# Layer-1 sparse-attention mixer rewritten: scores in fp32 on half arrays, four head-branches per unit, other fillers

## The chip, the core and the metric

One Trainium2 chip, of which the program uses one core. The metric is the device time of one execution in microseconds (us); the time before is 1038.02 us, the median of three runs (1037.85 to 1038.6). TensorE is called PE here, its weight loads PEld, VectorE DVE, ScalarE ACT, SyncE's DMA queue SP.

## The reference, cut to what matters

A two-layer decoder trunk in fp32 on 256 tokens of width 1024. Only the mixer of layer 1 changes:

```python
def mixer_nsa(h, in_w, cmp_pos, cmp_w1, cmp_w2, out_w, pos):     # 16 heads in 2 groups, head size 64
    u = h @ in_w
    q, kc, vc, ks, vs, kw, vw, gl = jnp.split(u, cuts, axis=-1)
    q_rope = rope_partial(q, pos)
    kcmp, vcmp = compress(kc, ...), compress(vc, ...)            # 15 compressed blocks
    gates = jax.nn.sigmoid(gl)                                   # three per head
    ...
    o_c = softmax(q @ kcmp, masked) @ vcmp
    o_s = softmax(q_rope @ rope(ks), causal) @ vs                # with 256 tokens all blocks are selected
    o_w = softmax(q_rope @ rope(kw), causal) @ vw                # and the window of 512 holds them all
    y = gates[0] * o_c + gates[1] * o_s + gates[2] * o_w
    return y @ out_w
```

So a head has two full causal branches ("selected" and "window") and one short compressed one. Around the mixer, in both layers, stand adaLN-modulated SwiGLU feed-forwards whose weights stream from HBM.

## The kernel before

All large products are done as three matmuls in fp32r (`mm3`, L154): each weight piece of 128x1024 is split by `Stream.step` (L76) into a high part `wh` (ACT, L86) and a rest `wl` (DVE, L90), each activation into HH and HL or yh and yl, and high x high, high x low and low x high are summed in PSUM. The split pieces lie in seven slots (`SPL_BUFS`), the raw ones in seven more. Attention products (`y<-pt,nvp`, transposes) are plain fp32; such a matmul shows as two PE instructions, called passes here, and two weight loads.

The tile framework orders the instructions of each engine itself from the order in the program and from what is ready; only blocks under `in_order()` keep the written order. `transition` (L371) is such a block: between two stages it finishes the last output columns of the stage before (`steps[b]`), updates x, and starts four projections of the next stage (`group(k)`: 12 matmuls) before the RMS sums are known; the sums go to PE after `lag` groups. It first asks (`st.need(p0 + 4)`) for five weight pieces of the next stage.

`mixer1` (L921) runs, in program order: the transition; the query projections 0 and 1 (`proj2`); the token projections (values and gates, into `vb`); rope of the keys and their split into kh and kl, stacked so that the contraction has 128 rows; the compression MLP (`hidden`), woven into the query projections 2 and 3; the rope of the queries and their split (`stack_q`, `place_q`); query projections 4 to 6; the compressed scores. Then comes `attention` (L615) over 32 jobs (8 head pairs i x 2 groups g x 2 branches), a software pipeline of five steps: `scores` (for a pair of jobs four fp32r matmuls of 256 and 512 columns over K=128, then a DVE custom instruction that adds the mask and takes the minimum, L626), `exps` (ACT, L634), `norm` (DVE, L643), `trans` (three PE transposes, L650, and a copy out of PSUM, L653 or L655) and `pv` (`y`, two fp32 matmuls of 256 and 128 columns). After four jobs `done` adds the compressed branch and hands y[i] to `OutProj`, whose 8 x 8 blocks of three matmuls are the filler between jobs (`op.some`), as are query projection 7 and the second half of the compressed branch (`todo`).

PSUM has eight banks: two oa and two ob accumulators, and four more, in attention three `ps` and one `y`. `mixer0` (L747) uses the same `attention` with fp32 scores over K=64 (`ps<-qf,qf`), one head after another.

Of the kernel before, what the change touches and what calls it, by code (L numbers as in the profile page):

```python
# [117 lines left out]
def hybrid_trunk_kernel(ctx: ExitStack, tc: tile.TileContext, xT, c, wst, mst, prm_d, cst_d, wab_d, cw1_d, cw2_d,  # L118
# [8 lines left out]
    banks4 = ExitStack()  # L127
# [9 lines left out]
    banks_for("psp", 4, 0)  # L137
# [10 lines left out]
    def ob():  # L148
        return accp.tile([P, 512], F32, tag="ob", name="ob")
# [302 lines left out]
    def ffn(name, l, i, prev):  # L452
# [83 lines left out]
        else:  # L536
# [143 lines left out]
    def rope(z, ap):  # L680
        rp = ob()
# [65 lines left out]
    def mixer0(prev):  # L747
# [12 lines left out]
        with tc.tile_pool(name="lru", bufs=1) as lp:  # L760
# [17 lines left out]
            def unrope(w):  # L778
                scatter(qf[w], rope(z[w], lp))
# [141 lines left out]
    def mixer1(prev):  # L921
# [8 lines left out]
        qf = [mp.tile([P, 4, S], F32, name=f"nqf{w}") for w in range(2)]  # L930
        kf = mp.tile([P, 2, S], F32, name="kf")
        kh = mp.tile([P, 2, 2, S], F32R, name="kh")
        kl = mp.tile([P, 2, 2, S], F32R, name="kl")
        vp = mp.tile([P, 2, 2, 192], F32, name="nvp")
        G.memset(vp[:, :, :, 64:128], 0.0)
# [8 lines left out]
        hid = [mp.tile([P, 2, 16], F32, name=f"hid{w}") for w in range(2)]  # L944
        for w in range(2):
            G.memset(hid[w], 0.0)
        G.memset(zk, 0.0)
        nc.sync.dma_start(out=cw2, in_=cw2_d)

        def do_q(i, b):  # L950
            A.activation(out=qf[i // 4][:, i % 4], in_=b, func=ACTF.Copy, scale=0.125)
            if i % 4 == 3:
                gather(zq[i // 4], qf[i // 4])

        with tc.tile_pool(name="cmp", bufs=1) as cp:
# [12 lines left out]
            kx = cp.tile([P, 2, S], F32, name="kx")  # L968
            for g in range(2):
                nc.sync.dma_start(out=kx[64 - 64 * g:128 - 64 * g], in_=kc[64 * g:64 * g + 64])  # L970
            for w in range(2):
                for g in range(2):
                    r = 64 * g + w
                    nc.sync.dma_start(out=zk[r:r + 61:4], in_=kf[64 * g:64 * g + 16, w])
            do_q(0, b0[:, 0:S])
            do_q(1, b1[:, 0:S])
            vb = [ps(), ps()]
            for q in range(3):
                wh, wl = st.need(p0 + 6 + q)
                for k in range(3 * q, min(3 * q + 3, KD)):  # L980
                    sl = slice((k - 3 * q) * 304, (k - 3 * q) * 304 + 304)
                    for t in range(2):
                        ts = slice(t * P, (t + 1) * P)
                        o = vb[t][:, 0:304]
                        mm(o, HH[:, k, ts], wh[:, sl], k == 0)
                        mm(o, HH[:, k, ts], wl[:, sl], False)
                        mm(o, HL[:, k, ts], wh[:, sl], False, k == KD - 1)
                st.free(p0 + 6 + q)
            for t in range(2):
                A.activation(out=gts[:, t], in_=vb[t][:, 256:304], func=ACTF.Sigmoid)  # L990
                src = vb[t][:, 0:256].rearrange("p (a e d) -> p a e d", a=2, e=2)
                dv = vp[:, t].rearrange("p a (b d) -> p a b d", b=3)[:, :, 0:3:2, :]
                A.activation(out=dv, in_=src, func=ACTF.Copy)
            preload(ACTF.Gelu_apprx_tanh, gts[:, 1, 0:1])
            zr = rope(zk, cp)
# [4 lines left out]
            for g in range(2):  # L1000
                a, b = slice(64 * g, 64 * g + 64), slice(64 - 64 * g, 128 - 64 * g)
                A.activation(out=kh[a, g], in_=kf[a], func=ACTF.Copy)
                A.activation(out=kh[b, g], in_=kf[a], func=ACTF.Copy)
                V.tensor_tensor(out=kl[a, g], in0=kf[a], in1=kh[a, g].bitcast(F32), op=ALU.subtract)
                V.tensor_tensor(out=kl[b, g], in0=kf[a], in1=kh[a, g].bitcast(F32), op=ALU.subtract)
            x2 = []
            for w in range(2):
# [10 lines left out]
                x2.append(t)  # L1018
            hb = [ps(), ps()]
# [5 lines left out]

            for w in range(2):
                b = oa()
                proj(p0 + 9 + w, b[:, 0:S], [lambda w=w, q=q: hidden(w, q) for q in range(8)])
                do_q(2 + w, b[:, 0:S])
# [6 lines left out]
        qs = [ap.tile([P, 2, 4, S], F32R, name=f"qs{w}", bufs=1) for w in range(2)]  # L1036

        def stack_q(w, i0, i1):
            for g in range(2):
                a, b = slice(64 * g, 64 * g + 64), slice(64 - 64 * g, 128 - 64 * g)  # L1040
                src, hi = qf[w][a, i0:i1], qs[w][a, g, i0:i1]
                A.activation(out=hi, in_=src, func=ACTF.Copy)
                V.tensor_tensor(out=qs[w][b, g, i0:i1], in0=src, in1=hi.bitcast(F32), op=ALU.subtract)

        def rope_q(w):
            zr = rope(zq[w], ap)
            zs = [ap.tile([P, S], F32R, tag=t, name=t, bufs=1) for t in ("zh", "zl")]
            split(*zs, zr)
            return zs

        def place_q(w, zs):
            for e in range(2):
                for n in range(2):
                    r = 64 * (e ^ n)
                    move(qs[w][r:r + 16, e].rearrange("p i t -> p (i t)"), zs[n][64 * e:64 * e + 64])

        scb = {}

        def cmp_scores(i):
            w = i // 4  # L1060
            if i % 4 == 0:
                scb[w] = ob()
# [4 lines left out]
        def cmp_soft(w):  # L1067
            sc = ap.tile([P, 2, 8, 16], F32, tag="sc", name="sc", bufs=2)
# [19 lines left out]
        def cmp_trans(w, sc):  # L1088
            pt = ps()
            scf = sc.rearrange("p t h c -> p (t h c)")  # L1090
            for t in range(2):
                PE.transpose(pt[:, t * P:t * P + P], scf[:, t * P:t * P + P], ident)
            A.activation(out=pc[w], in_=pt[:, 0:2 * P], func=ACTF.Copy)

        zs = rope_q(0)
        stack_q(0, 0, 2)
        stack_q(0, 2, 4)
        place_q(0, zs)
        b = oa()
        proj(p0 + 11, b[:, 0:S])  # L1100
        do_q(4, b[:, 0:S])
        bk = ps()
        mm(bk[:, 0:32], cw2[:, 0], hid[0].rearrange("p g c -> p (g c)"), True, True)
        for g in range(2):
            rows, cols = slice(64 * g, 64 * g + 64), slice(16 * g, 16 * g + 16)
            A.activation(out=kbd[rows, cols], in_=bk[rows, cols], func=ACTF.Copy)
        hid4 = ap.tile([P, 4, 32], F32, name="hid4", bufs=1)
        V.tensor_copy(out=hid4, in_=hid[1].rearrange("p g c -> p (g c)").unsqueeze(1).to_broadcast([P, 4, 32]))
        b = oa()
        proj(p0 + 12, b[:, 0:S])  # L1110
        do_q(5, b[:, 0:S])
        for i in range(4):
            cmp_scores(i)
        sc0 = cmp_soft(0)
# [4 lines left out]
        b = oa()  # L1119
        proj(p0 + 13, b[:, 0:S])  # L1120
        do_q(6, b[:, 0:S])
        late = {}

        def q7(k):
            if k == 0:
                late["b"] = oa()
                late["w"] = st.need(p0 + 14)
            b = late["b"][:, 0:S]
            mm3(b, at(late["w"], k), hk(k), k == 0, k == KD - 1)
            if k == KD - 1:  # L1130
                st.free(p0 + 14)
                do_q(7, b)
# [3 lines left out]

        todo = [lambda k=k: q7(k) for k in range(KD)] + [lambda: cmp_trans(0, sc0)]
        todo += [lambda i=i: cmp_scores(i) for i in range(4, 8)] + [lambda: None] * 6
        todo += [lambda: late.update(z=rope_q(1)), lambda: stack_q(1, 0, 2), lambda: stack_q(1, 2, 4), lambda: place_q(1, late["z"]), soft1, lambda: None, lambda: None, lambda: cmp_trans(1, late["sc"])]

        op = OutProj(p0 + 15, ap, 3)
        jobs = []
        cur = {}
        for i in range(8):
            for g in range(2):
                for br in range(2):
                    first, last = g == 0 and br == 0, g == 1 and br == 1

                    def ytile(i=i, first=first):
                        if first:  # L1150
                            cur[i] = ybank()
                        return cur[i]

                    def done(i=i):
                        b = cur.pop(i)
                        mm(b[:, 0:S], vb4[:, i % 4], pc[i // 4], False, True)
                        op.ready(i, b[:, 0:S])

                    def scores(i=i, g=g):
                        s0, s1 = ps(), ps()  # L1160
                        q = qs[i // 4][:, g, i % 4]
                        for n, k in enumerate((kh, kl)):
                            mm(s0[:, 0:2 * P].rearrange("p (b t) -> p b t", b=2), q[:, 0:P], k[:, g, :, 0:P],
                               n == 0, n == 1)
                            mm(s1, q[:, P:2 * P], k[:, g].rearrange("p b t -> p (b t)"), n == 0, n == 1)
                        return [(s0[:, b * P:(b + 1) * P], s1[:, b * S:(b + 1) * S]) for b in range(2)]

                    hd = 8 * g + i
# [197 lines left out]
```

## Time and profile before

| | us |
|---|---|
| median of three runs | 1038.02 |
| the profiled execution | 1037.28 |
| its span in the trace | 1035.5 |
| PE busy | 1000.6 (97%) |
| DVE busy | 816.9 (79%) |
| ACT busy | 565.3 (55%) |

A PE row's duration is from start to modelled end, with matmuls overlapping in the pipeline; what an instruction costs is the distance from its start to the next start. In a timeline row that merges xN instructions, the distance to the next row, divided by N, is that cost. The granted clock of PE is 1.00 where it runs at 2.4 GHz and 0.50 at 1.2 GHz. The layer-1 mixer takes from 700 us (its transition) to 835 us (the next stage's first group).

### The profile page before, as it was taken

The page shows a single profiled execution, that of the slowest core. Times are in us where ns is not written, and L with a number is a line of the kernel's source. Part 1 is how long each engine was busy: PE and PEld are TensorE (multiplying, and loading weights), DVE is VectorE, ACT ScalarE, POOL GpSimd, SP SyncE. Part 2 cuts the span into 40 slices and gives each one's busy share as a digit, 9 for nine tenths or more (in the row PEclk, how much of TensorE's full clock was granted, in tenths as well). Part 3 has the DMA queues.
Part 4 walks back from the last instruction along what each step waited for, and adds up shares of the span by engine and source line. Part 5 has one row for each costly group of instructions (what it writes and reads, how often), then busy time and mean ns, then how long its engine had stood idle before and what let it go on. Part 6 is the DMA issues. An engine that isn't in the chain of part 4 may idle for free. (4 is left out here: it accounts for less than half of the span.)

```text
span 1035.5 us, 20625 instructions
## 1 busy us (share of the span) xinstructions
PE 1000.6 (97%) x8070; PEld 974.6 (94%) x8070; DVE 816.9 (79%) x1584; ACT 565.3 (55%) x972; POOL 1.8 (0%) x15
## 2 busy tenths in 40 slices
PE   4999999999999999999999999999989999999996
PEld 2999999999789999999999999999978999999996
DVE  8979887889776988887689888859888678655554
ACT  5364343566976744444674444457777666444442
POOL 0000000000000000000000000000000000000000
PEclk9999999999999999999999999999989999999999
DMA  9979999947553599999439999962621117767611
GB/s 359 341 273 409 320 337 325 346 175 248 219 185 143 194 392 330 330 338 327 145 117 388 324 331 344 345 211 76 233 83 42 62 62 263 265 208 222 225 61 41
DMA packets 69795, 249.49 MB, mean 241 GB/s; under 512 B 8001, under 2 KB 9793, under 8 KB 69442
## 3 DMA queue, kind: packets, MB, share of 16 engines
q1 hardware_dynamic: 69410, 247.65, 67.6%
q8 instruction: 63, 1.03, 0.4%
q10 hardware_dynamic: 288, 0.52, 0.1%
q14 instruction: 34, 0.28, 0.1%
HBM read 245.39 MB, written 1.05 MB: 238 GB/s over the span
## 5 line engine op out<-in xcount | busy, mean ns | idle before, releaser
L90 DVE TENSOR_TENSOR wl<-raw,wh 128x1024 fp32r<-128x1024 f32 (+1 forms) x339 | 384.0, 1148 | 120.0 <-ACT wh L86 119.2
L86 ACT ACTIVATE wh<-raw 128x1024 fp32r<-128x1024 f32 x315 | 328.2, 1055 | 214.7 <-PE ps L152 103.4
L152 PE MATMUL ps<-HH,wh 128*128 128x256 f32 (+1 forms) x1392 | 392.2, 283 | 2.7 <-ACT HH L444 2.7
L152 PE MATMUL ps<-HH,wl 128*128 128x256 f32 (+1 forms) x1392 | 394.0, 283 | 0.8 <-DVE wl L90 0.7
L152 PE MATMUL ps<-HL,wh 128*128 128x256 f32 (+1 forms) x1392 | 392.8, 283 | 1.5 <-DVE HL L438 1.5
L152 PEld LDWEIGHTS ps<-HH,wh 128*128 128x128 f32 x1392 | 263.3, 190 | 4.2 <-ACT HH L444 3.6
L152 PEld LDWEIGHTS ps<-HH,wl 128*128 128x128 f32 x1392 | 264.4, 190 | 2.0 <-DVE wl L90 2.0
L152 PEld LDWEIGHTS ps<-HL,wh 128*128 128x128 f32 x1392 | 263.1, 189 | 2.3 <-DVE HL L438 2.0
L94 DVE SCALAR_TENSOR_TENSOR junk<-raw,cond 128x1024 bf16<-128x1024 f32 x144 | 175.7, 1220 | 12.3 <-DMA raw<-mst 12.1
L152 PE MATMUL oa<-gl,wh 128*128 128x256 f32 x352 | 98.1, 279 | 0.1
L152 PE MATMUL oa<-gh,wh 128*128 128x256 f32 x352 | 97.9, 279 | 0.1
L152 PE MATMUL ob<-gl,wh 128*128 128x256 f32 x352 | 97.7, 278 | 0.1
L152 PE MATMUL oa<-gh,wl 128*128 128x256 f32 x352 | 97.7, 278 | 0.0
L152 PE MATMUL ob<-gh,wh 128*128 128x256 f32 x352 | 97.6, 278 | 0.0
L152 PE MATMUL ob<-gh,wl 128*128 128x256 f32 x352 | 97.5, 277 | 0.0
L163 ACT ACTIVATE gh<-g 128x256 fp32r<-128x256 f32 x82 | 33.5, 416 | 69.1 <-DVE g L472 69.1
L152 PEld LDWEIGHTS oa<-gl,wh 128*128 128x128 f32 x352 | 66.2, 188 | 0.5 <-DVE gl L164 0.5
L152 PEld LDWEIGHTS oa<-gh,wh 128*128 128x128 f32 x352 | 66.2, 189 | 0.5 <-ACT gh L163 0.5
L152 PEld LDWEIGHTS ob<-gl,wh 128*128 128x128 f32 x352 | 66.1, 188 | 0.3 <-DVE gl L164 0.3
L152 PEld LDWEIGHTS oa<-gh,wl 128*128 128x128 f32 x352 | 66.3, 188 | 0.0
L152 PEld LDWEIGHTS ob<-gh,wh 128*128 128x128 f32 x352 | 66.0, 188 | 0.1
L152 PEld LDWEIGHTS ob<-gh,wl 128*128 128x128 f32 x352 | 66.1, 188 | 0.0
(231 smaller groups left out, 1375.6 us busy)
## 6 DMA issues: line engine op xcount, KB each, us to landing
raw<-wst SPq DMA_DIRECT2D x315, 512.0 KB, 5.2
raw<-mst SPq DMA_DIRECT2D x144, 512.0 KB, 5.4
cw<-cw SPq DMA_DIRECT2D x1, 2048.0 KB, 7.5
x<-xT SPq DMA_DIRECT2D x1, 1024.0 KB, 5.2
cst<-cst SPq DMA_DIRECT2D x1, 721.0 KB, 7.4
wab<-wab SPq DMA_DIRECT2D x1, 512.0 KB, 4.1
out<-raw ACTq DMA_DIRECT2D x2, 256.0 KB, 3.0
out<-raw SPq DMA_DIRECT2D x2, 256.0 KB, 2.7
```

The costliest lines, as they stand in the source:

```text
L86: nc.scalar.activation(out=h, in_=raw, func=ACTF.Copy)
L90: nc.vector.tensor_tensor(out=l[:, cols], in0=raw[:, cols], in1=h.bitcast(F32)[:, cols], op=ALU.subtract)
L94: nc.vector.scalar_tensor_tensor(out=self.junk, in0=raw, scalar=1.0, in1=self.cond, op0=ALU.mult, op1=ALU.mult, accum_out=self.modraw[i // ...
L152: PE.matmul(out, lhsT, rhs, start=start, stop=stop, skip_group_check=True)
L163: A.activation(out=h, in_=src, func=ACTF.Copy)
```

## The change

- **PSUM.** For the attention of layer 1 the two ob banks and the four ps banks are given up for one pool `att`: s0 and s1 of two banks each, pt and y of one, each a single buffer.
- **Scores.** One unit u is a head of each group with both branches, four head-branches. For each half t of the queries two fp32 matmuls over K=64 are issued, one on rows 0 to 63 (group 0) and one on rows 64 to 127 (group 1), each into its own bank, and two bf16 matmuls (identity x mask) add the causal mask. Queries are negated beforehand. One DVE minimum per half takes the place of the custom instruction; ACT reads the scores from PSUM. The splits kh, kl and qs, their copies and moves go.
- **Normalising and turning.** One DVE product per half; twelve transposes per unit in three steps of four through the one bank pt, copied by ACT (step 0) and DVE (steps 1, 2).
- **Values.** The zero padding of vp goes: each matmul gives 64 rows, group 0 on output partitions 0 to 63, group 1 on 64 to 127; nine per unit with the compressed branch.
- **Order.** Query projections 2 and 3 stand ahead of the token projections; `hidden` is woven into the latter. Query projections 4 to 7 become filler in the attention, then half of the output columns (accumulators 0 and 1). The other half (2 and 3, 96 matmuls) runs in `step` of the transition into the last feed-forward, whose `lag` goes from 4 to 2. The output weights are laid out by column block and half of k.

```diff
+    def banks_att():
+        banks4.close()
+        upper.close()
+        pool = banks4.enter_context(tc.tile_pool(name="att", bufs=1, space=bass.MemoryType.PSUM))
...
-                banks, rbs = transition(prev, amp, shift, p0, 3 if i == 0 else 4)
+                banks, rbs = transition(prev, amp, shift, p0, 3 if i == 0 else 4 - 2 * l)
...
         def do_q(i, b):
-            A.activation(out=qf[i // 4][:, i % 4], in_=b, func=ACTF.Copy, scale=0.125)
+            w = i // 4
+            A.activation(out=qf[w][:, i % 4], in_=b, func=ACTF.Copy, scale=-0.125)
             if i % 4 == 3:
-                gather(zq[i // 4], qf[i // 4])
+                gather(zq[w], qf[w])
+                for e in range(2):
+                    rows = slice(64 * e + 16, 64 * e + 64)
+                    nc.sync.dma_start(out=qr[w][rows], in_=qf[w][rows])
...
+        todo = [(1, None, lambda i=i, k=k: q_step(i, k)) for i in range(4, 8) for k in range(KD)]
+        todo += [(1, None, lambda: rope_q(1, ap, oa())), (2, None, cmp1), (0, None, soft1)]
+        outs = [(2, k, lambda b=b, k=k: out_step(b, k)) for k0 in (0, 4) for k in range(k0, k0 + 4) for b in range(2)]
+        todo += [(1, None, lambda: cmp_trans(1, late["sc"], oa()))] + outs
...
+        def scores(u, t):
+            s = att("s%d" % t, 2)
+            q = qr[u // 4][:, u % 4, t * P:(t + 1) * P]
+            for g in range(2):
+                rows = slice(64 * g, 64 * g + 64)
+                o = s[:, g, 0:2 * P * (t + 1)].rearrange("p (b k) -> p b k", b=2)
+                if t == 0:
+                    mm(o, q[rows], kf[rows, :, 0:P], True)
+                else:
+                    mm(s[:, g], q[rows], kf[rows].rearrange("p b k -> p (b k)"), True)
+            for g in range(2):
+                o = s[:, g, 0:2 * P * (t + 1)].rearrange("p (b k) -> p b k", b=2)[:, :, t * P:(t + 1) * P]
+                mm(o, identb, maskb, False, True)
+            return s
...
+        def turn(u, part):
...
+            pt = att("pt", 1)
+            for c in range(4):
+                PE.transpose(pt[:, c * P:(c + 1) * P], p[:, c, o:o + P], ident)
...
+        def values(u):
+            th, b = units[u]["th"], att("y", 1)
+            mm(b[:, 0:S], vb4[:, u % 4], pc[u // 4], True)
+            for br in range(2):
+                for kt in range(2):
+                    for g in range(2):
+                        rows = slice(64 * g, 64 * g + 64)
+                        rhs = th[:, 2 * g + br, 0:2].rearrange("p a t -> p (a t)") if kt == 0 else th[:, 2 * g + br, 2]
+                        mm(b[rows, kt * P:S], vp[:, kt, br, rows], rhs, False, br == 1 and kt == 1)
...
+        for u in range(KD):
+            more = 1 if u < 3 else 0
+            exps(u, 1)
+            if u + 1 < KD:
+                score(u + 1, 0)
+            filler(3 + more)
+            weights(u)
+            norm(u, 0)
+            if u + 1 < KD:
+                exps(u + 1, 0)
+                score(u + 1, 1)
+            turn(u, 0)
+            filler(2 + more)
+            norm(u, 1)
+            turn(u, 1)
+            turn(u, 2)
+            filler(3 + more)
+            values(u)
...
         def step(b):
-            op.step(b)
+            if b == 0:
+                filler(100)
+                assert not todo
+            if b > 1:
+                for k in range(KD):
+                    out_step(b, k)
```

## Rows read from the trace of the kernel before

**Rows 1.** The page: busy time of the engines, and the clock in 40 slices.
```profile
PE 1000.6 (97%) x8070; PEld 974.6 (94%) x8070; DVE 816.9 (79%) x1584; ACT 565.3 (55%) x972; POOL 1.8 (0%) x15
PEclk9999999999999999999999999999989999999999
```

**Rows 2.** Busy time by stretch (length, engines, clock, DMA share, GB/s): projections, attention.
```profile
713.03:755.59 42.56, 42.03 (x347) 41.61 (x345) 37.59 (x68) 34.89 (x59) 0.00 (x0) 1.00 0.49 167
...
755.59:765.00 9.41, 6.93 (x26) 5.07 (x26) 8.10 (x38) 5.20 (x19) 0.00 (x0) 0.64 0.54 184
755.59:827.60 72.01, 69.06 (x443) 60.97 (x443) 59.26 (x293) 50.10 (x172) 0.00 (x0) 0.95 0.20 65
```

**Rows 3.** PE's timeline at the attention's start: start, length, instructions, idle and releaser.
```profile
757.74 0.48 PE L152 MATMUL ps<-kh,qs 128*128 128x512 f32 x1 [1.08 <-DVE nm L626]
...
758.66 1.05 PE L152 MATMUL ob<-zq,cst 128*128 128x256 f32 x2
760.38 0.87 PE L650 MATMUL ps<-cst,p 128*128 128x128 f32 x3 [0.66 <-DVE p L643]
761.98 1.65 PE L152 MATMUL y<-pt,nvp 128*128 128x256 f32 x4 [0.74 <-DVE pt L653]
```

**Rows 4.** Busy time of one microsecond in that start, with the clock.
```profile
762.00:763.00 1.00, 1.00 (x3) 0.82 (x3) 1.00 (x8) 0.34 (x2) 0.00 (x0) 0.50 0.16 57
```

**Rows 5.** PE's groups by shape, 755.4 to 827.6 us: count, busy, mean ns, idle.
```profile
L152 PE MATMUL y<-pt,nvp 128*128 128x256 f32 x64 | 20.6, 404 | 0.9 <-DVE pt L653 0.7
L650 PE MATMUL ps<-cst,p 128*128 128x128 f32 x96 | 16.8, 284 | 0.7 <-DVE p L643 0.7
...
L152 PE MATMUL ps<-kh,qs 128*128 128x512 f32 x16 | 7.6, 473 | 1.2 <-DVE nm L626 1.1
L152 PE MATMUL oa<-yh,wh 128*128 128x256 f32 x24 | 7.3, 310 | 0.2 <-ACT yh L163 0.2
```

**Rows 6.** PE's timeline in dense stretches: fp32r of 512 columns, sixteen fp32 passes.
```profile
262.87 0.39 PE L152 MATMUL ps<-wl,HH 128*128 128x512 f32 x1
263.10 0.39 PE L152 MATMUL ps<-wh,HL 128*128 128x512 f32 x1
...
814.69 2.78 PE L152 MATMUL y<-pt,nvp 128*128 128x256 f32 x16
817.31 0.60 PE L152 MATMUL y<-pc,vb 128*128 128x256 f32 x2
```

**Rows 7.** PE's timeline in layer 0: transposes, scores over 64 rows, fp32r.
```profile
298.80 0.49 PE L650 MATMUL ps<-cst,p 128*128 128x128 f32 x3
299.22 0.92 PE L152 MATMUL ps<-qf,qf 64*128 64x128 f32 x4
300.07 0.39 PE L152 MATMUL oa<-yh,wh 128*128 128x256 f32 x1
300.30 0.28 PE L152 MATMUL oa<-yl,wh 128*128 128x256 f32 x1
300.42 0.28 PE L152 MATMUL oa<-yh,wl 128*128 128x256 f32 x1
```

**Rows 8.** DVE's groups by shape, 755.59 to 827.6 us.
```profile
L626 DVE CUSTOM_DVE_ANT_0 p<-ps,cst 128x256 f32<-128x256 f32 x32 | 13.2, 422 | 0.7 <-PE ps L152 0.4
...
L653 DVE COPY pt<-ps 128x384 f32<-128x384 f32 x6 | 3.3, 555 | 0.7 <-PE ps L650 0.6
```

**Rows 9.** The page: ACT's share of the weight split, all pieces.
```profile
L86 ACT ACTIVATE wh<-raw 128x1024 fp32r<-128x1024 f32 x315 | 328.2, 1055 | 214.7 <-PE ps L152 103.4
```

**Rows 10.** DVE's timeline in the transition into the last feed-forward.
```profile
830.44 1.29 DVE L90 TENSOR_TENSOR wl<-raw,wh 128x512 fp32r<-128x512 f32 x2 [1.93 <-ACT wh L86]
833.06 0.88 DVE L366 SCALAR_TENSOR_TENSOR x<-oa,modv,x 128x256 f32<-128x256 f32 x2 [1.33 <-PE oa L152]
```

**Rows 11.** PE's timeline there: the sums, and the first sweep after the groups.
```profile
840.87 0.50 PE L152 MATMUL ob<-over_d,sqs 128*128 128x1 f32 x4
...
851.08 0.28 PE L152 MATMUL ob<-HH,wh 128*128 128x256 f32 x1
851.83 0.38 PE L152 MATMUL ob<-HL,wh 128*128 128x256 f32 x1 [0.47 <-DVE HL L438]
```

More of the change, by code (lines that the diff above doesn't have):

```diff
@@ L148, in ob @@
     def ob():
-        return accp.tile([P, 512], F32, tag="ob", name="ob")
+        return psq["ob"].tile([P, 512], F32, tag="ob", name="ob")
     def mm(out, lhsT, rhs, start, stop=False):
@@ L974, in mixer1 @@
                     nc.sync.dma_start(out=zk[r:r + 61:4], in_=kf[64 * g:64 * g + 16, w])
+            kx = cp.tile([P, 2, S], F32, name="kx")
+            for g in range(2):
+                nc.sync.dma_start(out=kx[64 - 64 * g:128 - 64 * g], in_=kc[64 * g:64 * g + 64])
             do_q(0, b0[:, 0:S])
             do_q(1, b1[:, 0:S])
[L977 to L995, printed above, removed]
+            zr = rope(zk, cp, ob())
             for w in range(2):
@@ L999, in mixer1 @@
                     nc.sync.dma_start(out=kf[64 * g:64 * g + 16, w], in_=zr[r:r + 61:4])
[L1000 to L1005, printed above, removed]
+            for i in (2, 3):
+                b = oa()
+                proj(p0 + 4 + i, b[:, 0:S])
+                do_q(i, b[:, 0:S])
             x2 = []
@@ L1035, in mixer1, with cmp_scores @@
         ap = ap_.__enter__()
[L1036 to L1055, printed above, removed]
         scb = {}
-        def cmp_scores(i):
+        def cmp_scores(i, bank=None):
             w = i // 4
-            if i % 4 == 0:
-                scb[w] = ob()
+            if bank is not None:
+                scb[w] = bank
             for t in range(2):
@@ L1159, in scores @@
[L1159 to L1166, printed above, removed]
@@ L1168, in mixer1 @@
-                    hd = 8 * g + i
-                    jobs.append(dict(scores=scores if br == 0 else None,
-                                     v=lambda kt, br=br, g=g: vp[:, kt, br, 64 * g:64 * g + P],
-                                     y=ytile, first=first, last=False, gate=gts[:, :, 3 * hd + 1 + br],
-                                     done=done if last else None))
-        def filler(t):
-            for _ in range(2):
-                if todo:
-                    todo.pop(0)()
-            op.some(1 if t < 30 else 4)
@@ L1180, in mixer1, with weights @@
-        banks_for("att1", 3, 1)
-        attention(jobs, ap, filler)
+                    A.activation(out=p[:, 2 * g + br], in_=s[:, g, br * n:br * n + n], func=ACTF.Exp, scale=-1.0,
+                                 bias=nm[:, g, br:br + 1], accum_out=units[u]["sm"][:, t, g, br:br + 1])
+        def weights(u):
+            sm = units[u]["sm"]
+            V.reciprocal(out=sm, in_=sm)
+            for t in range(2):
+                gt = gts[:, t].rearrange("p (g i c) -> p g i c", g=2, c=3)[:, :, u, 1:3]
+                V.tensor_tensor(out=sm[:, t], in0=sm[:, t], in1=gt, op=ALU.mult)
@@ new lines, in mixer1 @@
+        score(0, 0)
+        exps(0, 0)
+        score(0, 1)
+        cmp_trans(0, sc0, att("pt", 1))
+        filler(8)
+        for u in range(KD):
[16 more added lines that the diff above has]
+            values(u)
```

173 lines of the change are left out of this document (114 added, 59 removed).

## The prediction

> **What bounds the kernel now.** I read the page first: PE is busy 97% of the span at full clock nearly everywhere, DVE 79%, ACT 55% [rows 1]. Busy PE is not PE at its peak, so the second view is the busy time by stretch: in the projections (713 to 756 us) PE has no gap to speak of, in the attention of layer 1 (72.0 us) it shows 69.1 us busy, and its first 9.4 us have 6.9 us and a clock of 0.64 [rows 2]. The third view is the distance from start to start, which gives each kind of instruction its price:
>
> - an fp32r matmul of 256 columns 0.12 us (300.30 to 300.42) [rows 7], of 512 columns 0.23 us [rows 6];
> - sixteen fp32 passes, eight of 256 and eight of 128 columns, 2.62 us, so 0.217 and 0.11 us [rows 6], and 0.43 us for 512 columns, an estimate by doubling;
> - a transpose of 128 columns 0.11 us. Three of them, ahead of scores over 64 rows, take 0.42 us, which is 0.09 us more; the four 64-row passes behind them take 0.85 us where 0.22 + 0.43 = 0.65 would do, and the next fp32r matmul 0.23 us in place of 0.12 [rows 7]. So one visit to a part of the array costs 0.09 + 0.20 + 0.11 = 0.40 us beside its passes.
>
> At these prices the attention stretch holds 64 x (0.217 + 0.11) = 20.9 us of values, 16 x 2 x (0.12 + 0.23) = 11.2 of scores, 100 transposes 11.0 (96 of them in the group, four of the compressed branch) [rows 5], 16 passes of the compressed branch 3.5, one rope 0.4, and 131 output matmuls 15.7 (six groups of 20 to 24, of which the largest is shown [rows 5]): 62.7 us. The stretch lasts 72.0 us [rows 2], so PE waits 9.3 us in it. The 26 instructions of the first 9.4 us [rows 2] come to some 3.7 us at these prices, so 5.7 us of the waiting fall there: there is no filler yet, PE waits for the minimum, the normalised weights and the copy of the first jobs [rows 3], and then works for six microseconds at 0.50 of its clock, the 1.2 GHz level [rows 4]. The other 3.6 us are spread over 62 us. **So PE's work bounds this stage, and its waits are the 9.3 us that a better order can win.**
>
> **The change part by part**, against the profiled execution (1037.28 us, 1.8 us more than its span; the median of the runs is 0.7 us above it).
>
> *Scores.* Per unit: four fp32 products over 64 rows, two passes each, four passes of 256 and four of 512 columns. The trace never shows products of the two row halves next to each other, so what they cost together is bounded: one after another 4 x 0.217 + 4 x 0.43 = 2.59 us, wholly in pairs 1.29 us. PE's rows run in program order, and both passes of group 0 stand ahead of those of group 1; then only the second of group 0 and the first of group 1 can share the array, three lengths of four: 1.94 us, which I take. The Trainium skill (TensorE: Matmul & The Clock Gate, Part 3: Packing small matmuls) says that matmuls on different row groups overlap, about 4 ns from start to start, but start and end in program order; no run here shows it, and by it the sum would be the same 1.94. Four mask matmuls add 0.48 us at the fp32r price. Before, two g-pairs cost 1.4 us per unit.
>
> *Values.* Eight products of 64 output rows, 2.62 us one after another, 1.31 in full pairs. Here groups alternate product by product, so a second pass overlaps the next product's first throughout: 1.61 us by the same reasoning. The compressed branch stays at 0.43 us, the twelve transposes at 1.32.
>
> *Visits.* Scores of each half and the values each enter and leave a part of the array: three visits, of which values and the next unit's first scores are adjacent in program order; so 2 to 3 times 0.40 us, 0.8 to 1.2. I take 0.8, since the values' weight loads are half as wide as those of the rows.
>
> *Sum.* 1.94 + 0.48 + 1.61 + 0.43 + 1.32 + 0.8 = 6.58 us per unit, 52.6 for eight, with the compressed transposes (0.44) and one rope (0.43) 53.5 us. Before, the same work without output matmuls was 62.7 - 15.7 = 47.0. **PE's work rises by 6.5 us.**
>
> *Waits that go.* The 32 steps of query projections 4 to 7 (96 matmuls, 11.5 us) are ready when attention starts, and 96 output matmuls follow as y[k] come. That covers the start, so I take the 5.7 us as gone, and of the remaining 3.6 I leave 1.0: everywhere but in the first three units enough filler is ready, and the order of the framework takes what is ready. Bounds: 0 and the present 9.3. If the start is not covered, 5.7 us come back. So 9.3 - 1.0 = 8.3 us are won.
>
> *DVE and ACT.* 64 custom minima (422 ns for 256 columns [rows 8]) with their accumulator reads become 16 minima over the same columns; 16 large copies of 512 columns (0.69 us each, by the 384-column copy of 555 ns and about a nanosecond per further column) replace six. Both stay under the 59 and 50 us that they have now in 72 [rows 2], the splits kh, kl and qs are gone, and ACT keeps 64 exponentials. I cost this at nothing; PE's 76.5 us of work in the new stage, 53.5 + 23 of fillers, cover it. What is late next is the chain through the single buffers, a rival below.
>
> *Projections.* The same matmuls in another order; 0. Two query projections (5.8 us) now cover the keys' rope and the copies for the compression, which the long token projections covered before.
>
> *DMAs.* Two gathers stay, four copies of qf to qr come, eight moves of the split queries go. They stand on SP between weight loads and wait for `do_q`; behind them queue those loads, for which DVE's and ACT's splits wait. DMA is busy 20% here [rows 2]; 0.
>
> *Transition into the last feed-forward.* 48 output matmuls of column pair 2 and 48 of pair 3 run in it, 5.8 us each. `st.need` at its head now demands nine pieces, four output pieces and five of the feed-forward, with seven slots: the last one's split waits for the second piece of pair 2 and stands on DVE and ACT ahead of every update of x. From that release ACT needs 1.06 us [rows 9] and DVE 1.29 us [rows 10] for the split, and then DVE the chain from the first update (833.06 [rows 10]) to the sums (840.87 [rows 11]), 7.8 us: 10.2 us. PE has 5.8 us of pair 3 and two groups of 1.44 us, 8.7 us, ahead of the sums: it waits 1.5 us. In return the sums come two groups earlier relative to the sweep that follows; the gaps there (one of them 0.75 us from start to start, 851.08 to 851.83, for a matmul of 0.12 [rows 11]; 1.4 us in all) should go. Net 0, between -1.4 and +1.5.
>
> **Sum.** 1037.3 + 6.5 - 8.3 + 0 = 1035.5 us for the profiled execution, **1036.2 us** on the median's scale. Two large terms cancel, so the sign hangs on how the halves pair and on the new waits.
>
> **The rivals.**
>
> *Full pairs (1028.6 us).* If passes of the two halves run wholly side by side, scores fall by 0.65 and values by 0.30 us per unit, 7.6 us. Against it stands the order of the passes; for it, that nothing in the trace forbids it. The Trainium skill (TensorEngine Tiling (Array Packing), Theoretical Speedup) gives up to a factor of two for half arrays; by that the time would be this one.
>
> *No pairs (1049.6 us).* The change would not do what it says: 0.65 + 1.01 us per unit more, 13.4 us. For it: 64-row passes cost as much as full ones plus a visit [rows 7].
>
> *Single buffers (1041.7 us, slower).* `turn(u, 1)` and `turn(u, 2)` are adjacent and share pt: the second waits for a DVE copy of 0.69 us, and `values` for another. If filler does not fill them, that is up to 1.4 us per unit, 11 us; half of it, 5.5, gives 1041.7. It decides from 0.5 us per unit on (3.9 us over eight units, up to 2.1 us above the time before). PE's clock would make it worse, since after the gaps at 756 to 758 us it fell to 0.50 [rows 3, 4]. Against it: behind the start, with one y bank and a three-deep ps, the present order loses only 3.6 us.
>
> **How the numbers follow.** Forecast 0.44 (own range 1032 to 1041), full pairs 0.26, single buffers 0.14, no pairs 0.13, else 0.03. About 0.2% (2.1 us) is what a measurement of this kernel tells from no change. Faster: 0.19 of the forecast's share, 0.26 of full pairs and 0.01 of the rest, that is 0.46; the same: 0.14 of the forecast's and 0.02 of single buffers', 0.16; slower: 0.11 of the forecast's, 0.12 of single buffers', 0.13 and 0.02, that is 0.38. The range reaches from below full pairs to just short of no pairs: 1027 to 1049.5.
>
> **What would show it.** Start-to-start distances of `s0`, `s1` and `y` passes: pairs 4 to 30 ns apart for the second of one group and the first of the next prove the three quarters, 0.217 and 0.43 throughout prove no pairs. The stretch from the first score to the last y should lose its half-clock part and its waits at the start; PE's waits should name neither pt's copies nor the minima above 0.5 us per unit; at the sums of the last transition a wait of 1 to 2 us on DVE should stand, and the sweep behind it none. The forecast is wrong if scores leave the expected 1.94 us per unit in either direction, or if filler runs out before unit 7.

## The result and the profile after

The changed kernel takes **1049.01 us** (median of four runs, 1048.54 to 1050.54), the kernel before beside it 1037.93; the ratio is 1.0108 with a 95% interval of 1.009 to 1.0125. It is **slower by 11 us**, where 1036.2 was forecast. The profiled execution took 1049.2 us, 11.9 more than that of before. The page's rows that answer to [rows 1]:

```profile
PE 1007.5 (96%) x8102; PEld 961.2 (92%) x8102; DVE 806.8 (77%) x1380; ACT 550.5 (53%) x943; POOL 1.6 (0%) x14
PEclk9999999999999999999999999999989999999998
```

PE is no less busy, DVE and ACT are less. The extra time lies in one stage, from the first projection of the mixer to the first group of the next stage. Busy time by stretch, the whole of that stage in the kernel before:

```profile
713.03:835.02 121.99, 118.50 (x849) 110.00 (x847) 100.65 (x368) 89.45 (x237) 0.00 (x0) 0.97 0.31 106
```

and in the changed kernel, whole and in five parts (projections, first units, a stretch without filler, the rest, the last output products):

```profile
712.54:847.43 134.89, 126.81 (x880) 97.31 (x879) 91.88 (x167) 75.46 (x209) 0.00 (x0) 0.97 0.30 99
712.54:749.83 37.29, 35.41 (x286) 34.46 (x284) 26.01 (x50) 24.36 (x41) 0.00 (x0) 1.00 0.51 172
749.83:776.60 26.77, 26.20 (x161) 16.02 (x161) 22.35 (x39) 17.93 (x66) 0.00 (x0) 1.00 0.27 95
776.60:790.84 14.24, 11.90 (x58) 7.97 (x57) 8.73 (x22) 4.61 (x17) 0.00 (x0) 0.76 0.30 84
790.84:833.50 42.66, 39.92 (x270) 25.94 (x271) 26.49 (x44) 19.75 (x75) 0.00 (x0) 1.00 0.08 25
833.50:847.43 13.93, 13.37 (x114) 12.93 (x111) 8.29 (x14) 8.81 (x13) 0.00 (x0) 1.00 0.47 148
```

The stage is 12.9 us longer. It can be split three ways: idle time (length less PE's busy time), time lost to the clock (busy time x (1 - granted clock), summed over windows of one microsecond), and the rest, PE's work at full clock. Before: 3.5 + 2.7 + 115.8 us; after: 8.1 + 3.4 + 123.4. **So 7.6 us are more work, 4.6 more idle time and 0.7 more clock loss.** All kernels of this study in the same split (the median is over all runs, the other columns are of the profiled execution):

| kernel | median, us | stage | idle | clock | work |
|---|---|---|---|---|---|
| before | 1037.9 | 122.0 | 3.5 | 2.7 | 115.8 |
| after | 1049.0 | 134.9 | 8.1 | 3.4 | 123.4 |
| e1, all pairs | 1045.6 | 130.1 | 13.3 | 0.0 | 116.8 |
| e2, no pairs | 1053.7 | 137.9 | 7.5 | 0.0 | 130.4 |
| e3, other banks | 1055.3 | 139.1 | 8.6 | 5.9 | 124.5 |
| e4, e1 and e3 | 1055.0 | 138.1 | 15.6 | 5.8 | 116.7 |
| e5, e1 with half copies | 1059.6 | 149.7 | 16.6 | 15.4 | 117.7 |
| e6, first order by hand | 1045.9 | 139.3 | 11.0 | 13.6 | 114.7 |
| e7, e1 with copies by ACT | 1047.1 | 129.7 | 11.8 | 1.7 | 116.2 |
| e8, lag 3 | 1048.9 | 134.9 | 8.2 | 3.4 | 123.3 |
| e9, second order by hand | 1036.6 | 132.1 | 5.7 | 12.0 | 114.5 |
| e10, projections | 1045.3 | 130.5 | 6.9 | 1.6 | 121.9 |
| e11, e9 + e10 + lag 3 | **1033.1** | 119.6 | 3.6 | 1.7 | 114.3 |
| e12, e11 without pairs | 1053.7 | 139.2 | 3.4 | 8.5 | 127.3 |

The profiled executions of e5, e6 and e9 had the clock at 0.50 for some 24 us ahead of the attention, 12 us of their clock loss; by their times only two of e5's four runs, one or two of e6's five and two of e9's twelve are like that, so the stage of e6 and e9 is longer here than the median says (e9 profiled: 1049.8 us).

**Where the work comes from.** PE's timeline of the changed kernel; a row with x4 holds both passes of both groups, one with x2 those of one group:

```profile
749.83 0.70 PE L169 MATMUL s<-kf,nqr 64*128 64x256 f32 x4
750.46 0.39 PE L169 MATMUL s<-maskb,identb 128*128 128x256 bf16 x2
750.78 1.13 PE L169 MATMUL s<-kf,nqr 64*128 64x512 f32 x4
751.85 0.39 PE L169 MATMUL s<-maskb,identb 128*128 128x256 bf16 x2
...
762.95 0.60 PE L1215 MATMUL pt<-cst,p 128*128 128x128 f32 x4
763.48 0.65 PE L169 MATMUL y<-th,nvp 128*64 128x256 f32 x4
764.06 1.12 PE L169 MATMUL s<-kf,nqr 64*128 64x512 f32 x2
765.11 1.09 PE L169 MATMUL y<-th,nvp 128*64 128x128 f32 x12
766.13 1.12 PE L169 MATMUL s<-kf,nqr 64*128 64x512 f32 x2
767.19 0.39 PE L169 MATMUL s<-maskb,identb 128*128 128x256 bf16 x2
```

From start to start both groups together take 1.07 us (750.78 to 751.85), and one group alone 1.05 us (764.06 to 765.11). Side by side the second group is free; cut apart the pair costs double, and one more entry into the half array. In single starts, the first passes of the two groups are 5 to 7 ns apart, and so are their second passes. Of 32 pairs of passes 14 run so: in 9 of the 16 halves the framework put something between the two groups. Scores and masks take 25.5 us by the starts of their 64 + 32 instructions.

**Where the waiting is.** The stretch without filler:

```profile
776.40 0.60 PE L169 MATMUL y<-pc,vb 128*128 128x256 f32 x2
777.93 0.66 PE L1215 MATMUL pt<-cst,p 128*128 128x128 f32 x4 [0.93 <-ACT th L1218]
779.18 0.67 PE L169 MATMUL oa<-zq,cst 128*128 128x256 f32 x2 [0.59 <-DMA zq<-nqf]
779.68 3.12 PE L169 MATMUL oa<-kbd,nqf 128*128 128x32 f32 x16
782.61 1.09 PE L1215 MATMUL pt<-cst,p 128*128 128x128 f32 x4
783.63 2.92 PE L169 MATMUL y<-th,nvp 128*64 128x256 f32 x16
```

and in windows of one microsecond (the third number from the end is the clock):

```profile
778.83:779.83 1.00, 0.65 (x5) 0.63 (x5) 0.82 (x2) 1.00 (x5) 0.00 (x0) 1.00 0.88 213
779.83:780.83 1.00, 1.00 (x9) 1.00 (x7) 0.42 (x1) 0.25 (x2) 0.00 (x0) 0.61 0.91 266
780.83:781.83 1.00, 1.00 (x7) 1.00 (x6) 0.00 (x0) 0.00 (x0) 0.00 (x0) 0.50 0.96 315
```

After two waits (0.93 and 0.59 us) the clock falls to 0.50 among the sixteen matmuls of 32 columns and stays there for seven microseconds: the sixteen value passes, which take 1.6 us in the two pieces above (763.48 to 764.06 and 765.11 to 766.13), take 2.85 here (783.63 to 786.48). No query product is left, and the first output product stands at 790.84, behind the compressed branch that holds its bank.

### The profile page after: what moved, and what is told of

The parts are those of the page before. It is cut to its first block, busy times and chain, and to the rows that moved or that the text cites. A ratio compares the mean times of both kernels' runs of the same rounds, so it can differ in the third digit from the quotient of the medians.

```text
span 1047.2 us, 20415 instructions
## 1 busy us (share of the span) xinstructions
PE 1007.5 (96%) x8102; PEld 961.2 (92%) x8102; DVE 806.8 (77%) x1380; ACT 550.5 (53%) x943; POOL 1.6 (0%) x14
## 3 DMA queue, kind: packets, MB, share of 16 engines
HBM read 245.39 MB, written 1.05 MB: 235 GB/s over the span
## 4 chain that ended last, share of the span: by engine, by line
PE 80%; DVE 10%; ACT 6%; issue 2%; DMA 1%; SPq 0%; ACTq 0%; DVEq 0%
PE ps L169 45%; PE oa L169 17%; PE ob L169 14%; DVE wl L90 2%; PE s L169 2%; PE y L169 2%; ACT wh L86 1%; DVE junk L94 1%; DVE t L460 1%; DVE HL L455 1%; PE pt L1215 1%; DVE x L383 1%; ACT HH L461 1%; DMA raw<-mst 1%; ACT p L1193 1%
## 5 line engine op out<-in xcount | busy, mean ns | idle before, releaser
L90 DVE TENSOR_TENSOR wl<-raw,wh 128x1024 fp32r<-128x1024 f32 (+1 forms) x339 | 384.0, 1147 | 119.6 <-ACT wh L86 118.6
```

What stands on the lines that cost most here:

```text
L90: nc.vector.tensor_tensor(out=l[:, cols], in0=raw[:, cols], in1=h.bitcast(F32)[:, cols], op=ALU.subtract)
```

## The experiments

Most of them set PE's order. Every matmul of the attention is recorded under a letter as it is written, and each is made to follow its predecessor in a list; `S0`, `S1` are the score products of a half (two, one per group), `M0`, `M1` the masks, `T` transposes, `V` and `Vc` values, `q` and `o` query and output products, and `*n` counts matmuls. DVE and ACT remain with the framework.

```diff
+        prev = None
+        for item in ORDER.split():
+            c, n = item.split("*")
+            for _ in range(int(n)):
+                i = seqs[c].pop(0)
+                if prev is not None:
+                    tc.add_manual_dep(i, prev.name, ...)
+                prev = i
```

**e1: all pairs side by side.** The list is the order that the trace of the changed kernel shows, with such edits at nine places:

```diff
-T*4 V*2 S1*1 V*6 S1*1 M1*2 T*4
+T*4 V*8 S1*2 M1*2 T*4
```

> The changed kernel with PE's order of the attention written out: the same order, except that the two score products of a half (group 0 on the upper, group 1 on the lower rows of the array) and their two masks always stand side by side, at the place where the second of them stood. In the changed kernel 9 of the 16 halves have something between the two (4 of half 0, 5 of half 1). Theory A (split pairs): alone, each member takes its full 0.63 us (half 0) or 1.05 us (half 1) instead of sharing it, and a further entry into the half array 0.15 us; 4 x 0.77 + 5 x 1.20 = 9.1 us less than the changed kernel, 1040 us. Rival B (starved stretch): PE waits anyway for copies and banks from 776 to 791 us, the split scores only fill waits, and the time stays at 1046 to 1049 us.

1045.55 us (ratio to before 1.0074, 1.0058 to 1.0089): 3.5 us less than the changed kernel, not 9. The work fell by 6.6 us (scores and masks from 25.5 to 17.0 us), and in the profiled execution the 3.4 us of clock loss went too, but 5.2 us came back as idle time. PE at the place shown above, where the value products stood around a score:

```profile
763.55 0.65 PE L174 MATMUL y<-th,nvp 128*64 128x256 f32 x4
764.85 1.09 PE L174 MATMUL y<-th,nvp 128*64 128x128 f32 x12 [0.64 <-DVE th L1243]
```

The score had filled a wait for the copy out of the single bank pt. The waits of PE for these copies (us, times, longest) in the changed kernel

```profile
PE pt L1215 <- DVE th L1220: 1.5, 2, 0.8
PE pt L1215 <- ACT th L1218: 1.2, 2, 0.9
PE y L169 <- DVE th L1220: 0.2, 1, 0.2
```

and in e1:

```profile
PE y L174 <- DVE th L1243: 3.1, 6, 1.0
PE pt L1237 <- ACT th L1241: 1.9, 3, 0.9
PE pt L1237 <- DVE th L1243: 1.7, 2, 0.9
```

From 2.9 to 6.7 us. So a third theory, **C**: the framework, which takes what is ready, cuts pairs where PE would have to wait for pt, and whoever joins the pairs must put other work there.

**e2: no pairs.** The changed kernel's order, with each mask right behind its own score; where a pair was still whole:

```diff
-S0*2 M0*2 S1*2 M1*2
+S0*1 M0*1 S0*1 M0*1 S1*1 M1*1 S1*1 M1*1
```

> The opposite dose: PE's order of the changed kernel, but the mask of each group stands right behind its own score product, so that no two score products are neighbours any more; the 7 halves that were side by side (4 of half 0, 3 of half 1) are split as well. Theory A: 4 x 0.77 + 3 x 1.20 = 6.7 us more than the changed kernel, 1055.7 us. Rival B: within 2 us of the changed kernel, 1047 to 1051 us.

1053.65 us (1.0134 to 1.0165), 4.6 more than the changed kernel: 7.0 us more work, 0.6 less idle, and no clock loss in the profiled execution. From all pairs (e1) to none, scores and masks rise from 17.0 to 31.3 us, the work of the stage by 13.6 and the time by only 8.1, because 5.8 us of idle time go.

**e3: other banks for the compressed branch.**

```diff
-            b = oa()
+            b = att("y", 1)
...
-        todo += [(1, None, lambda: rope_q(1, ap, oa())), (2, None, cmp1), (0, None, soft1)]
+        todo += [(1, None, lambda: rope_q(1, ap, att("y", 1))), (2, None, cmp1), (0, None, soft1)]
...
-        todo += [(1, None, lambda: cmp_trans(1, late["sc"], oa()))] + outs
+        todo += [(1, None, lambda: cmp_trans(1, late["sc"], att("pt", 1)))] + outs
```

> The changed kernel with the rope of the queries 4 to 7, their compressed scores and the compressed transposes in the banks of y (the first two) and pt (the last) instead of oa, so that both oa banks are free for the output products as soon as query projection 7 has been copied out; nothing else. Theory B (starved stretch): from 776.6 to 790.8 us PE has some 7.4 us of work at full clock in 14.2 us, because the filler has run out and the output products wait behind the compressed branch for its two banks; with them free the 6 to 7 us go: 1042 to 1043 us. Theory A (split pairs alone): the pairs stay split as before, the waits move elsewhere, 1047 to 1049 us.

1055.27 us (1.015 to 1.018): slower by 6, which neither theory said. The output products do come earlier (778.00), but the compressed transposes now stand in pt's row, and all turns behind them:

```profile
789.12 0.66 PE L1094 MATMUL pt<-cst,sc 128*128 128x128 f32 x2 [2.81 <-DVE sc L1088]
```

The stall had moved, and with it the clock was at 0.50 from 787.3 to 801.0 us (5.9 us lost). **e4: both edits.**

> Both edits: banks of y and pt for the second half of the compressed branch, and all score pairs and masks side by side. If A and B are both true and add up: 1049 - 9 - 6.5 = 1033.5 us. If the two are the same time counted twice (split scores fill the waits): 1040 to 1043 us.

1054.98 us (1.0148 to 1.0218), over both expectations: the work of e1 (116.7 us) with 15.6 us idle. The two did not add up; neither puts anything into the waits.

**e5: copies in halves.** Only beside e1's list:

```diff
-            if part == 0:
-                A.activation(out=units[u]["th"][:, :, part], in_=src, func=ACTF.Copy)
-            else:
-                V.tensor_copy(out=units[u]["th"][:, :, part], in_=src)
+            A.activation(out=units[u]["th"][:, 0:2, part], in_=src[:, 0:2], func=ACTF.Copy)
+            V.tensor_copy(out=units[u]["th"][:, 2:4, part], in_=src[:, 2:4])
```

> The kernel with all score pairs side by side (e1: 1045.5 us, PE gaps of 12.7 us in the attention, 6.7 us of them on the copies out of the one pt bank), same PE order; each of the 24 copies of 512 columns out of pt is cut into two of 256, one by ACT and one by DVE side by side, so that the bank comes free some 0.25 us sooner. Theory C (the single pt bank sets the pace where PE waits): 11 waits on these copies, 0.25 us each, and the chain behind them: 2 to 4 us less than e1, 1041.5 to 1043.5 us. Rival (PE's work bounds, or DVE as a whole): within 1 us of e1, or slower by the 16 further instructions on ACT.

1059.61 us (1054.12 to 1064.08), slower than e1 and not the gain that was expected; from the first score to the end of the stage it takes 101.4 us where e1 takes 92.8. PE waits 12.3 us for DVE's halves alone (longest 2.1), where e1 waits 6.7 for all copies. My reading, which no run isolates: each turn now needs a place in two queues, and what counts is not the copy's length but what stands ahead of it. In e1, DVE and then PE:

```profile
812.51 1.83 DVE L1228 TENSOR_TENSOR p<-p,sm 128x512 f32<-128x512 f32 x2
814.25 0.69 DVE L1243 COPY th<-pt 128x512 f32<-128x512 f32 x1
```
```profile
812.82 0.60 PE L1237 MATMUL pt<-cst,p 128*128 128x128 f32 x4
813.35 0.65 PE L174 MATMUL y<-th,nvp 128*64 128x256 f32 x4
814.99 0.44 PE L174 MATMUL y<-th,nvp 128*64 128x128 f32 x4 [0.99 <-DVE th L1243]
```

The copy of a turn that was done at 813.4 begins at 814.25, behind the two normalisations of the next unit. **e7: all copies by ACT** (one line in place of the four taken out above), e1's list:

> The kernel with all score pairs side by side (e1: 1045.5 us), same PE order, with one line changed: all three copies out of pt go by ACT (0.60 us each) instead of one by ACT and two by DVE, where in e1 they stand behind products of 0.69 to 1.2 us that normalise the next unit, or behind minima. Theory C1 (the waits on pt are places in DVE's queue): the 4.8 us of PE's waits for DVE's copies in e1 become shorter than 2 us, 1042 to 1044 us. Rival C2 (the copies wait in whichever queue they are in; ACT has blocks of four exponentials of 1.4 and 1.8 us): as long as e1 or longer, 1045 to 1049 us.

1047.05 us (1.0071 to 1.0149). Rival C2 holds: the waits are on ACT now (4.4 + 1.2 us, longest 1.8), 5.6 us where e1 has 6.7. So neither queue is free of instructions that stand ahead of a copy, and cover on PE is what remains.

**e6 and e9: orders by hand.** The compressed branch is in y's bank, the pairs are joined. One unit in e6 and in e9:

```diff
-T*4 o*6 T*4 o*3 T*4 o*3 Vc*1 V*8 S0*2 M0*2 S1*2 M1*2
+T*4 o*6 T*4 S0*2 M0*2 T*4 o*6 Vc*1 V*8 S1*2 M1*2
```

> PE's order of the attention written out by hand: score pairs and masks side by side and 18 query products earlier in the queue than in the changed kernel; between the three turns of a unit, and between the last turn and the values, stand 3 to 6 filler products (0.35 to 0.7 us) each, so that the copy out of the single pt bank runs beside them; the rope of queries 4 to 7, their compressed scores and compressed transposes use y's bank, so that the output products have the oa banks from query projection 7 on. Work of PE from the first query filler (741.5 us) at the prices of the trace: 96 query and 84 output products 21.4 us, eight units of 5.7 us (scores 1.69, masks 0.48, transposes 1.31, compressed 0.43, values 1.30, entries 0.45) 45.3 us, second half of the compressed branch 2.9 us: 69.6 us, so the attention could end at 811 us instead of 833.5. Theory C (waits on pt, filled by split pairs): most of the 22 us go; with 6 to 10 us of waits left 1032 to 1037 us, so faster than the kernel before. Rival (the chain of a unit over DVE and ACT bounds, whatever stands between): the waits come back at other places, 1042 to 1046 us.

e6: 1045.91 us (1043.31 to 1057.33), which is the rival's figure. Idle time fell only to 11.0 us; the waits on pt's copies are 4.1 us, in nine pieces of up to 0.9: three matmuls (0.35 us) do not cover a copy (0.60 us on ACT, 0.69 on DVE).

> The second hand-written PE order (the first, e6: 1043.3 to 1050 us, PE gaps 8.3 us in the attention, 2.4 of them before the first transposes and most others of 0.34 to 0.94 us at the second and third turn of a unit): 30 query products behind the first scores instead of 18, a pair of scores (0.9 us) as cover between the second and third turn, six fillers (0.7 us) ahead of the second and of the values. Theory C (single pt bank with its copies): gaps of the attention fall from 8.3 to 3 to 5 us, fastest runs 1039 to 1041 us. Rival (the chain over DVE and ACT bounds): gaps stay at 7 to 9 us, 1043 us and more. In either case PE's work in it stays at 80 to 82 us, so that it does not get clearly below the kernel before.

e9: 1036.62 us, ratio 1.0 (0.9979 to 1.0022). The same work as e6 within 0.2 us, idle 5.7, and for pt's copies 1.3 us. **Theory C holds for the waits on pt**, and the time came out lower than expected. Of the 5.2 us of idle time that went, 2.8 are those waits; most of the rest is 1.7 us of waits for the first exponentials (ahead of two scores, up to 770 us), where e9 puts 36 query products ahead of the first transposes in place of 21. In the profiled run, one of the two longest among twelve (1049.8 and 1053.7 us), the clock was at 0.50 from 732.7 to 756.6 us, in the projections, whose waits the edits of e10 take out.

**e8: lag 3 in the last transition.**

```diff
-                banks, rbs = transition(prev, amp, shift, p0, 3 if i == 0 else 4 - 2 * l)
+                banks, rbs = transition(prev, amp, shift, p0, 3 if i == 0 else 4 - l)
```

> The changed kernel with one more group of projections ahead of the sums in the last transition (lag 3 instead of 2), nothing else. The changed kernel waits 1.4 us for the squares there, and its sweep behind has no gaps (5.6 us, before 7.2 us). Forecast theory (the lag sets both): the wait of 1.4 us goes into the group (1.44 us) and some of the sweep's gaps come back: 1047.6 to 1049 us. Rival (the wait is pure loss): 1047.3 us or less, with a sweep as short as now.

1048.92 us (1.0094 to 1.0162), the same as the changed kernel. The sums of the changed kernel

```profile
851.86 0.61 PE L169 MATMUL ob<-over_d,sqs 128*128 128x1 f32 x4 [1.40 <-DVE sqs L356]
```

wait 1.40 us after two groups; with lag 3 they wait for nothing and stand at the same distance from the first group (4.4 us). The group fills the wait, no more.

**e10: the projections.** PE's waits there in the changed kernel:

```profile
720.10 0.39 PE L169 MATMUL oa<-HH,wh 128*128 128x256 f32 x1 [0.92 <-ACT nqf L969]
...
727.91 1.05 PE L169 MATMUL ps<-x,cw 128*128 128x30 f32 x8 [0.81 <-issue]
```

```diff
             proj2(p0 + 4, p0 + 5, b0[:, 0:S], b1[:, 0:S])
+            do_q(0, b0[:, 0:S])
+            do_q(1, b1[:, 0:S])
...
-            do_q(0, b0[:, 0:S])
-            do_q(1, b1[:, 0:S])
...
-                    hidden(k // 4, 2 * (k % 4))
-                    hidden(k // 4, 2 * (k % 4) + 1)
+                    for n in range(0 if k < 3 else 16 * (k - 3) // 5, 0 if k < 3 else 16 * (k - 2) // 5):
+                        hidden(n // 8, n % 8)
```

> The changed kernel with two edits ahead of the attention: the copies of query projections 0 and 1 out of their banks stand ahead of the keys' on ACT, and the compression matmuls are woven into the last five of the eight steps of the token projections instead of all eight. In the changed kernel PE has gaps of 1.9 us in this stage (0.92 and 0.8 us in the trace, for that copy and for the compression's inputs), before 0.5 us; in several runs of the other variants the clock fell to 0.50 behind them for 20 us. Theory D (the new order of the projections costs 1.4 us and more): 1047 to 1048 us. Rival (the gaps move on to the attention's start, where the keys are ready at the same time as now): 1048.5 to 1049.5 us.

1045.28 us (1.0053 to 1.0081), 3.7 less than the changed kernel: both waits are gone and the first score starts 34.6 us after the first projection instead of 37.3. Not all of the 3.7 is the projections': the framework ordered the attention anew as well, with 18 pairs of passes whole in place of 14, and the stage has 1.5 us less work and 1.8 less clock loss. **e11: e9, e10 and e8 together.**

> The second hand-written PE order (e9, most runs 1035.4 to 1038.7 us, two of twelve 1049.8 and 1053.7 us with the clock at 0.50 from 733 to 755 us) with the two edits ahead of the attention of e10, and lag 3 in the last transition, which puts a group in the place of PE's 1.4 us wait for the sums. Theory D: the stage ahead of the attention loses 1 to 2 us, the clock stays at 1.00 in it: 1033.5 to 1035.5 us in nearly all runs. Rival (those gaps only move on): 1036 to 1037 us, with the slow-clock runs still among them.

**1033.11 us** (1032.77 to 1033.82), ratio 0.995 (0.9937 to 0.9964): a little faster than expected, and faster than both kernels. PE in one unit:

```profile
784.72 0.60 PE L1246 MATMUL pt<-cst,p 128*128 128x128 f32 x4
...
786.07 0.66 PE L1246 MATMUL pt<-cst,p 128*128 128x128 f32 x4
786.66 0.70 PE L182 MATMUL s<-kf,nqr 64*128 64x256 f32 x4
787.29 0.39 PE L182 MATMUL s<-maskb,identb 128*128 128x256 bf16 x2
787.52 0.64 PE L1246 MATMUL pt<-cst,p 128*128 128x128 f32 x4
...
789.24 1.52 PE L182 MATMUL y<-th,nvp 128*64 128x256 f32 x16
790.69 1.13 PE L182 MATMUL s<-kf,nqr 64*128 64x512 f32 x4
```

**e12: e11 without pairs** (the edit of e2).

> The order of e11 (1033.1 us; gaps of 2.6 us in the attention) with one edit: the mask of each group stands right behind its own score product, so that no two score products are neighbours. With e1 and e2 the same step, from all pairs to none, added 13.4 us to the scores, 1.0 us to the masks and 8.1 us to the time, because PE's gaps fell from 11.4 to 5.6 us. In e11 scores and masks take 18.6 us, in e2 31.4 us. Theory (a split pair is paid in full where PE has no waits left that it could fill): 12.8 us more work, at most 1 us of it back out of the gaps, 1045 to 1046 us. Rival (half of it is absorbed here too): 1039 to 1041 us.

1053.69 us (1.012 to 1.0155): 20.6 us more than e11, and 8 above the expectation. The work rose by 13.0 us, as expected, with no idle time to take it up (3.6 us before, 3.4 after); 6.8 more are clock loss, which the expectation did not hold (last section). Where PE waits, a lost pair costs a part of its price (e1 to e2: 8.1 us for 13.6 us of work); where it doesn't, all of it.

## Why the prediction was wrong

- **The failed step is "Waits that go".** It took 8.3 us off, and from the first score to the end of the stage idle time and clock loss rose by 4.0 (from 5.6 to 9.6): this term alone is 12.3 us off, where the profiled execution is 13.7 off (1049.2 against 1035.5). The projections add 1.4 and PE's work 1.1; the rest of the kernel gives 1.0 back. Three errors are in the term. (1) The 9.3 us of the stage before were not all waits: PE was idle 2.95 us of the 72.0 [rows 2] and lost 2.7 to the clock; the other 3.7 are busy time above the prices taken, and no run shows that an order wins them. (2) "The 32 steps ... are ready when attention starts": the framework had used 51 of their 96 matmuls before the first score, so the filler ended at 775 us, and the output products were barred until 790.84 by the compressed branch in their banks. The start's stall did go (idle 0.6 us from 749.83 to 776.60, clock 1.00), and a like one stands further on: 2.3 us idle and 3.4 of clock from 776.60 to 790.84. So filler was missing in units 2 and 3, where the prediction itself named filler that "runs out before unit 7" as a sign of being wrong. (3) DVE and ACT: "I cost this at nothing", from their busy time. Their queues matter, not their share: a copy of 0.69 us that stands behind 1.83 us of normalisation holds pt, and PE with it (e1; in e5 and e7 too the waits stay).
- **PE's work, +6.5 forecast, +7.6 measured**, is right in size for the wrong reason, which is luck. Pairs are complete, not three quarters: in e1 scores and masks take 17.0 us, where 19.4 were counted, and the whole work is only 1.0 us above before. But a program order is not the queue's order; with 9 of 16 halves cut, 25.5 us result. The three quarters took both passes of one group to stand ahead of the other group's; the trace shows the two first passes together, then the two second ones, so an order of starts does not keep the groups apart. The Trainium skill (TensorE: Matmul & The Clock Gate, Part 3: Packing small matmuls) gives about 4 ns from start to start for tiles in different row groups; the 5 to 7 ns here are close to it.
- *Visits*: in e11 scores, masks and values with their entries take 3.9 us per unit (18.7 + 12.2, by eight) against 4.8 forecast (1.94 + 0.48 + 1.61 + 0.8). The last transpose ahead of a score pair is 0.09 us longer than one inside a row, the pair's first pass 0.10 and its last 0.09: 0.3 us per visit where 0.4 was taken. The Trainium skill (TensorEngine Tiling (Array Packing), Tiling Modes) says that a change of mode drains the engine; these longer distances fit it, though they do not show the drain itself.
- *Values*: 1.52 us per unit in e11 (12.2 by eight), and their visit is in it; 1.61 without a visit were counted, because the second pass was taken to overlap only in part.
- *Projections 0*: wrong by 1.4 us of idle time (0.5 to 1.9).
- *Last transition, net 0*: right. The wait at the sums is 1.40 us (1.5 forecast), and from the first group to the end it took 199.8 us against 200.5; e8 exchanges wait for group.
- **The rivals.** *No pairs* named 1049.6 us, nearly the result, by luck: the array does pair, the order cut 9 of 16 score halves, and waits made up the rest; really no score pairs is 1053.7 (e2). *Full pairs* was right on the array, but its 1028.6 us is 4.5 below even e11. *Single buffers* named the waits on pt (up to 11 us; e1 has 6.7), and not that the framework would fill them by cutting pairs, so that the changed kernel shows only 2.9.

## What to carry to other kernels

A pair of half-array matmuls saves its half only while both stand next to each other in the engine's queue, so look at the queue's order, not the program's, and pin it. Before a stall is counted as won, list which filler is really left at that point and which banks it needs; and for a single buffer count the longest instruction that can stand ahead of its copy, then put work of that length on the bound engine. The same arithmetic was worth +11 or -5 us by the order and, for the compressed branch, the bank alone.

## What the runs showed of the hardware

**The clock fell behind short waits, and once with PE busy.** e12 was at 0.50 twice. First from 747.2 to 757.4 us (5.1 us lost), behind a wait of 0.8 us ahead of the first score:

```profile
745.00:746.00 1.00, 0.36 (x3) 0.17 (x2) 1.00 (x2) 0.30 (x1) 0.00 (x0) 1.00 1.02 418
746.00:747.00 1.00, 0.86 (x4) 0.41 (x4) 1.00 (x3) 0.00 (x0) 0.00 (x0) 1.00 1.02 418
747.00:748.00 1.00, 1.00 (x4) 0.36 (x3) 0.88 (x2) 0.09 (x1) 0.00 (x0) 0.62 0.33 131
```

e11 has the same wait and was at 0.50 from 747.0 to 750.4 us only (1.7 us lost). The second time (3.4 us lost), busy time in three stretches:

```profile
793.00:795.00 2.00, 2.00 (x14) 1.50 (x13) 0.95 (x3) 1.50 (x8) 0.00 (x0) 1.00 0.00 0
795.00:801.00 6.00, 6.00 (x19) 3.59 (x18) 2.46 (x5) 2.24 (x8) 0.00 (x0) 0.50 0.00 0
801.00:804.00 3.00, 3.00 (x17) 1.94 (x16) 1.77 (x6) 0.60 (x4) 0.00 (x0) 0.86 0.00 0
```

PE is recorded as busy throughout, and its last wait, of 0.43 us, ended at 788.0; ahead of the fall stand compressed scores of 32 columns and one group's score alone in half of the array. The clock then stays at 0.50 (1.2 GHz) for nearly seven microseconds. e2, with as few pairs but other neighbours, kept 1.00 in the whole stage. Why one and not the other stays open.

**In the projections the same waits did and did not bring it.** Behind idle times of 0.9 and 0.8 us the profiled execution of e9 was at 0.50 for 24 us; the changed kernel's, with the same two waits, kept 1.00 there. Ten of e9's twelve runs took 1035.4 to 1038.7 us and cannot hold such a stretch, which costs 12. In e11, where those two waits are gone, all five runs lie within 1.1 us of each other.
